# One more couple of up-projection blocks shares its P2 product, operand sums are queued behind weight splits, and the last norm's sums are gathered one product before their matmul

## The chip, the cores and the metric

The kernel runs on one core of a Trainium2 chip. The metric is the time of one execution in device microseconds (us). Before the change the median of three runs is 917.64 us (916.22 to 918.17).

## What is computed

One layer of a decoder trunk over 1024 tokens of width 1024, in float32. A normalised input goes through a projection into a pooling mixer and a gated recurrence, an output projection follows, then a squared-ReLU MLP of width 4096, a gated embedding, and a last norm:

```python
h = h + jnp.concatenate([y_pool, y_lru], axis=-1) @ w_out[l]
z = rms_norm(h, norm_mlp_g[l])
h = h + jnp.square(jax.nn.relu(z @ w_up[l])) @ w_down[l]
z = rms_norm(h, norm_ple_g[l])
gate = jax.nn.sigmoid(z @ w_ple_gate[l] + b_ple_gate[l])
h = h + gate * (p[l] @ w_ple_proj[l])
return rms_norm(h, norm_final_g)
```

The change lies in `z @ w_up` (the up-projection) and in the norm ahead of `w_ple_gate`.

## The kernel before

**Precision.** Each float32 operand is split into a rounded upper part (ScalarE, ACT in the profile, line L189) and a lower part, the remainder (VectorE, DVE, line L190). A product is three matmuls per block: upper by upper, upper by lower, lower by upper. A matmul that reads a lower part waits for its L190.

**The up-projection** is done in 16 blocks m = 0 to 15 of 256 output columns. Each block is a 2 by 2 block product by a seven-product scheme (Strassen's with Winograd's sums): P1 to P7, each 12 matmuls of 512 columns on 4 blocks of 128. P1 and P2 use the operands `y_wide`, P3 uses `y`, P4 to P7 use `a`. Two products of neighbouring blocks can again be made together by the same scheme, with halves: seven small products of 6 matmuls of 256 columns each (`sub_product`, L1020), in place of two products of 12 matmuls of 512. In the code this is a couple: `DOUBLES` lists the first blocks of the couples that make P4 together (3, 5, ... 13), `LATERS` those that make P2 together (6, 8, 10, 12). The second block of a couple runs `up_double`, in which the small products are woven between the block's own; all other blocks run `up_pair` with whole products.

A couple needs sums of its token operands (`double_operand`, L983 and L986, on DVE) and their splits, made once for all couples: n = 3, 1, 2 and 4, for P4 out of `a` and for P2 out of `y_wide`. Number 4 overwrites a quarter of the operand itself, so no whole P2 (or P4) can run behind it until it is restored. It also needs sums of its weights: for P4 in `double_weight`, for P2 in `later_sums`, which is issued behind the split of P6 of the couple's first block.

**What sets the order.** Python issues instructions with priorities, and a scheduler lays down one fixed order for each engine before the run. `issue_after(x)` keeps what is issued under it behind the instruction x in that order; `lowest[0]` is the newest lower split. Each engine then works through its own queue in order. The weights of a product live in four tiles (two tags of two buffers), so a weight can be split only when the product four weights before it has been made.

**The end of the kernel** (n = 0 to 7 in the loop over output blocks, first half of the tokens): each n is a projection of 6 matmuls and a gate of 24. The norm of the second half is made on the way. `Norm.add` squares and adds the 8 blocks, `Norm.gather` transposes and reduces them on DVE and splits the small result (L506, L507, L508, L509), one matmul by a block matrix spreads the sums (L519, written to `n2b_ps`), and `Norm.rstd` takes them on. Weights of the gate for blocks 4 to 7 are loaded into `wg_raw` and split on the same engines, into `a`.

Of the kernel before, what the change touches and what calls it, by code (L numbers as in the profile page):

```python
# [49 lines left out]
NPAIR = DFF // P // 2  # L50
# [14 lines left out]
def block_kernel(  # L65
# [48 lines left out]
    R = fixed("rstd", F32)  # L114
    start = pool.tile([P, 6 * S + NVEC + NT * S + 64], F32, name="t_h")
    t_all = start[:, : 6 * S].rearrange("p (i s) -> p i s", i=6)
    T = [t_all[:, i] for i in range(6)]
# [18 lines left out]
    def bank(name):  # L136
        return pd.tile([P, HALF], F32, tag="pd", name=name)
# [46 lines left out]
    lowest, upper = [], []  # L184
# [80 lines left out]
    FIRST_UP = "P6", "P7", "P4", "P5", "P1", "P2", "P3"  # L265
    UP = [(0, kind) for kind in FIRST_UP]
    DOUBLES = range(3, NPAIR - 1, 2)
    LATERS = range(6, NPAIR - 2, 2)

    def doubled(m):  # L270
        return "P4" if m - 1 in DOUBLES else "P2" if m - 1 in LATERS else None
# [4 lines left out]
    for m in range(1, NPAIR - 1):  # L276
        if doubled(m):
            n = second_alone(m)
# [678 lines left out]
    def copy(to, ps, fn=AF.Copy):  # L957
        nc.scalar.activation(by(to, ps), got(ps), fn)
# [30 lines left out]
    def double_operand(k, n):  # L989

        b11, b12, b21, b22 = ([f32(x) for x in quadrant(k, i, j)] for i in range(2) for j in range(2))
        to = apart(E[1][:, SECOND] if k == "P4" else H[6][:, FIRST])
        if n == 3:
            total(to, ((1, b12[0]), (-1, b22[0]), (1, b12[1]), (-1, b22[1])))
            split(to, *extra_parts(k, 0))
        elif n == 1:
            total(to, ((1, b11[0]), (-1, b12[0]), (1, b11[1]), (-1, b12[1])))
            split(to, *extra_parts(k, 1))
        elif n == 2:
            total(to, ((1, to), (1, b22[0]), (1, b22[1])))  # L1000
            split(to, *extra_parts(k, 2))
        else:
            total(to, ((-1, to), (1, b21[0]), (1, b21[1])))
            split(to, *quadrant(k, 0, 1))
# [86 lines left out]
    def up_fourth(m):  # L1091
# [4 lines left out]
        finish_up(m, cc)  # L1096
        leave_up()

    def up_double(m, k):

        before, own = (up_sums(x)[3 if k == "P4" else 1] for x in (m - 1, m))
# [21 lines left out]
        nc.scalar.activation(by(own[:, right], z[:, right]), got(z[:, right]), AF.Copy, scale=-1.0)  # L1123
        up_product(m, "P6", b, more=True)
        copy(c12, b)
        x = bank(f"ps_x_u{m}")[:, left]
        sub_product(k, x, w54[1], 4)
        copy(own[:, left], x)
# [32 lines left out]
    def up_pair(m):  # L1161
        if doubled(m):
            return up_double(m, doubled(m))
        cc, c11, c12, c21, c22 = up_sums(m)
        a, d = up_open(m)
        b = chains[m]
        leave_up()
        if m > DOUBLES[0]:
            pass
        elif m > 1:  # L1170
            up_fourth(m - 1)
        else:
            norm.rstd(R, [x for hs in HALVES for x in norm.sums(hs)], square=True)
            leave("hl")
            extra["P4"].extend(space("x", 2, F32R))
        up_product(m, "P6", b, more=True)
        copy(c12, b)
        if m > DOUBLES[0]:
            finish_up(m - 1, up_sums(m - 1)[0])
        up_product(m, "P2", a, more=True)  # L1180
        copy(c11, a, AF.Relu)
        for k, ns in (("P4", ((), (3,), (1, 2), (4,))), ("P2", ((), (), (), (3,), (), (1, 2, 4)))):
            for n in ns[m] if m < len(ns) else ():
                double_operand(k, n)
        up_product(m, "P3", d, more=True)
        take(c12, d, c12)
        if m == 1:
            finish_up(0, up_sums(0)[0])
            leave_up()
        up_product(m, "P7", b, more=True)  # L1190
        take(c22, b, c22)
        if m in DOUBLES:
            copy(c21, chains.pop(m))
# [202 lines left out]
    norm2 = Norm("n2", T[0], T[1:2])  # L1396
# [224 lines left out]
    for g, hs in enumerate(GROUPS):  # L1621
# [3 lines left out]
        for n, o in enumerate(ORDER[g]):  # L1625
# [21 lines left out]
            if g == 0 and n > 0:  # L1647
                for o in range(NT) if n == 1 else ():
                    norm2.add(H[o], SECOND)
                if n == 3:  # L1650
                    norm2.rstd(R, norm2.sums(SECOND, T[2][:, SECOND]))
                for o in LATER[n - 1]:
                    ple_in_normed(o, SECOND)
            if g == 1:
# [143 lines left out]
```

## Time and profile before

| what | value |
|---|---|
| median of 3 runs | 917.64 us (916.22 to 918.17) |
| the profiled execution, its own time | 918.25 us |
| its span, first to last instruction | 916.4 us |
| mean granted TensorE clock | 0.997 |
| busy: TensorE (PE) | 906.0 us, 99% |
| busy: VectorE (DVE) | 737.0 us, 80% |
| busy: ScalarE (ACT) | 514.2 us, 56% |
| stage of the up-projection, from the PE's rows | 224.97 to about 511 us |

A row of a timeline gives the start, the length, the engine, the line, the operation, what is written and read, the shape, how many instructions the row merges, and in brackets how long the engine sat idle before it and what ended that. Matmuls overlap, so the price of one is the distance from start to start, not its length. PEld is the weight load of the PE, which goes ahead of its matmul.

### The profile page before, as it was taken

Reading aid. Unit: us, or ns where it says so; the run is one execution under the profiler, and the core shown is the slowest. Engines: PE = TensorE matmul, PEld = TensorE weight load, DVE = VectorE, ACT = ScalarE, POOL = GpSimd, SP = SyncE. Lnnn points to the kernel's source line nnn. Section 1 sums busy time; section 2 is a strip of 40 time slices with the busy share of each in tenths; the row PEclk is TensorE's granted clock in tenths of the full one; section 3 lists DMA queues with packets and bytes.
Section 4 is the critical chain, followed back from the end, with each engine's and each line's share of the span. In section 5 each row is a group of like instructions: output and inputs, shape, how many; then the busy total and the mean of one; then the engine's idle time right before and its main releaser. Section 6 shows DMA issues by size and latency. Waiting matters only on the chain.

```text
span 916.4 us, 11820 instructions
## 1 busy us (share of the span) xinstructions
PE 906.0 (99%) x4401; PEld 794.0 (87%) x4401; DVE 737.0 (80%) x1004; ACT 514.2 (56%) x683; POOL 51.9 (6%) x76
## 2 busy tenths in 40 slices
PE   9999999999999999999999999999999999998996
PEld 7888888888888989999998888888888888887886
DVE  7999974668998667887887877799777589898876
ACT  6569892447565656666767554564343346475323
POOL 4400001000000000000000000000001001100001
PEclk9999999999999999999999999999999999999999
DMA  8210145435478667778685988366535355331353
GB/s 274 101 47 28 63 150 151 150 92 174 112 188 254 173 204 195 204 233 203 190 242 180 359 312 293 116 218 197 201 97 136 129 167 119 70 100 62 93 173 135
DMA packets 60328, 150.88 MB, mean 165 GB/s; under 512 B 5360, under 2 KB 10352, under 8 KB 60272
## 3 DMA queue, kind: packets, MB, share of 16 engines
q1 hardware_dynamic: 54288, 136.77, 45.3%
q0 software_dynamic: 4752, 12.59, 8.3%
q10 hardware_dynamic: 1232, 0.79, 0.4%
q8 instruction: 34, 0.56, 0.2%
q14 instruction: 22, 0.18, 0.1%
HBM read 110.27 MB, written 39.85 MB: 164 GB/s over the span
## 4 chain that ended last, share of the span: by engine, by line
PE 93%; DVE 4%; issue 1%; DMA 1%; ACT 0%; POOLq 0%; POOL 0%; ACTq 0%; DVEq 0%
PE ps_P_d L447 31%; PE ps_i L447 9%; PE ps_o L447 9%; PE ps_b_u L447 8%; PE ps_d_u L447 8%; PE ps_a_u L447 6%; PE ps_e L447 5%; PE ps_l L447 3%; PE ps_z_u L1020 3%; PE ps_e L1533 2%; PE ps_P_u L447 2%; PE ps_v_u L1020 1%; PE ps_l L644 1%; PE ps_x_u L1020 1%; PE ps_g L713 1%
## 5 line engine op out<-in xcount | busy, mean ns | idle before, releaser
L447 PE MATMUL ps_P_d<-a,wd_P_hi 128*128 128x512 f32 x880 | 261.7, 379 | 0.0
L447 PEld LDWEIGHTS ps_P_d<-a,wd_P_hi 128*128 128x128 f32 x880 | 166.3, 189 | 23.6
L447 PE MATMUL ps_P_d<-a,wd_P_lo 128*128 128x512 f32 x440 | 166.8, 379 | 0.0
L447 PEld LDWEIGHTS ps_P_d<-a,wd_P_lo 128*128 128x128 f32 x440 | 83.2, 189 | 11.8
L222 DVE TENSOR_TENSOR t_h<-t_h 128x512 f32<-128x512 f32 (+2 forms) x104 | 72.6, 708 | 14.1 <-ACT t_h L925 13.0
L190 DVE TENSOR_TENSOR wu_P<-t_h,wu_P 128x512 fp32r<-128x512 f32 x86 | 58.7, 686 | 30.8 <-ACT wu_P L189 30.7
L447 PE MATMUL ps_b_u<-a,wu_P 128*128 128x512 f32 x360 | 82.4, 379 | 0.0
L447 PEld LDWEIGHTS ps_b_u<-a,wu_P 128*128 128x128 f32 x360 | 66.6, 189 | 8.6
L190 DVE TENSOR_TENSOR a<-wd,a 128x1024 fp32r<-128x1024 f32 x56 | 67.3, 1220 | 2.3 <-ACT a L189 2.0
L189 ACT ACTIVATE wu_P<-t_h 128x512 fp32r<-128x512 f32 x86 | 53.3, 624 | 24.0 <-DVE t_h L222 10.6
L447 PE MATMUL ps_i<-a,wi_hi 128*128 128x512 f32 x256 | 66.1, 381 | 0.0
L189 ACT ACTIVATE a<-wd 128x1024 fp32r<-128x1024 f32 x56 | 58.3, 1051 | 9.3 <-PE ps_P_d L447 6.5
L899 DVE TENSOR_TENSOR t_h<-t_h,ps_P_d 128x512 f32<-128x512 f32 (+1 forms) x48 | 37.1, 772 | 30.5 <-PE ps_P_d L447 30.5
L447 PE MATMUL ps_a_u<-y_wide,wu_P 128*128 128x512 f32 x264 | 60.6, 379 | 0.0
L447 PEld LDWEIGHTS ps_a_u<-y_wide,wu_P 128*128 128x128 f32 x264 | 49.7, 189 | 7.0
L447 PEld LDWEIGHTS ps_i<-a,wi_hi 128*128 128x128 f32 x256 | 48.1, 189 | 8.0 <-PE ps_g L713 0.3
L189 ACT ACTIVATE wd_P_hi<-wd 128x1024 fp32r<-128x1024 f32 x24 | 25.3, 1054 | 50.0 <-PE ps_P_d L447 47.9
L447 PE MATMUL ps_d_u<-a,wu_P 128*128 128x512 f32 x180 | 41.3, 379 | 0.0
L447 PE MATMUL ps_d_u<-y,wu_P 128*128 128x512 f32 x180 | 41.3, 379 | 0.0
L447 PE MATMUL ps_i<-a,wi_lo 128*128 128x512 f32 x128 | 38.1, 379 | 0.0
L190 DVE TENSOR_TENSOR wd_P_lo<-wd,wd_P_hi 128x1024 fp32r<-128x1024 f32 x24 | 29.3, 1221 | 10.1 <-ACT wd_P_hi L189 10.1
L447 PEld LDWEIGHTS ps_d_u<-a,wu_P 128*128 128x128 f32 x180 | 33.3, 189 | 4.3
(307 smaller groups left out, 1731.8 us busy)
## 6 DMA issues: line engine op xcount, KB each, us to landing
wd<-act SPq DMA_DIRECT2D x56, 512.0 KB, 5.7
act<-t_h SPq DMA_DIRECT2D x48, 512.0 KB, 4.9
t_h<-in_w_up SPq DMA_DIRECT2D x30, 512.0 KB, 5.2
wd<-in_w_down SPq DMA_DIRECT2D x16, 512.0 KB, 6.7
t_h<-in_w_up POOLq DMA_DIRECT2D x15, 512.0 KB, 7.1
t_h<-in_xT SPq DMA_DIRECT2D x14, 512.0 KB, 4.6
wg_raw<-in_w_gate SPq DMA_DIRECT2D x10, 512.0 KB, 3.2
wi_raw<-in_w_in SPq DMA_DIRECT2D x9, 512.0 KB, 3.2
```

Of the source, the lines that this page charges most:

```text
L189: first = pin(nc.scalar.activation(hi, src, AF.Copy))
L190: lowest[:] = [pin((eng or nc.vector).tensor_tensor(lo, src, f32(hi), ALU.subtract)).ins]
L222: return nc.vector.tensor_tensor(to, x, y, op).ins
L447: ins = nc.tensor.matmul(ps, w, turns(z[:, hs]), start=first and z is zhi and w is whi, stop=last and w is wlo, skip_group_check=more,)
L644: nc.tensor.matmul(ps, kblk(w, o), turns(z[:, hs]), start=k == n == 0, stop=False)
L713: nc.tensor.matmul(x, w[r, o * P : (o + 1) * P], turns(z[r, at : at + HALF]), start=n == 0, stop=n == 2)
L899: (eng or nc.vector).tensor_tensor(to, to if y is None else y, x, ALU.add)
L1020: nc.tensor.matmul(ps, kblk(w, t), turns(z[:, t]), start=t == x == 0 and not more, stop=t == 1 and x == 2, skip_group_check=more,)
L1533: nc.tensor.matmul(pg, z, turns(quad[x == 1][:, k]), start=n == 0, stop=n == 3 * NT - 1, skip_group_check=True)
```

## The change

`LATERS` begins at 4 instead of 6, so that blocks 4 and 5 make P2 together as well: block 5 goes through `up_double` instead of `up_pair`, and blocks 4 and 5 have no whole P2 of their own. The operand sums for P2 have to be there two blocks earlier: n = 3 and 1 are made in block 3, n = 2 and 4 in block 4 (before: 3 in block 3, the rest in block 5). All operand sums, those of P4 too, are now issued behind the newest lower split. In the end stage the gather of the second norm's sums is issued at n = 2, its matmul stays at n = 3.

```diff
-    LATERS = range(6, NPAIR - 2, 2)
+    LATERS = range(4, NPAIR - 2, 2)
...
+    MADE = {"P4": {1: (3,), 2: (1, 2), 3: (4,)}, "P2": {3: (3, 1), 4: (2, 4)}}
+
+    def double_operands(m):
+
+        for k, ns in MADE.items():
+            for n in ns.get(m, ()):
+                with tc.issue_after(lowest[0]):
+                    double_operand(k, n)
+
     def up_double(m, k):
...
         up_product(m, "P6", b, more=True)
         copy(c12, b)
+        double_operands(m)
         x = bank(f"ps_x_u{m}")[:, left]
...
         up_product(m, "P2", a, more=True)
         copy(c11, a, AF.Relu)
-        for k, ns in (("P4", ((), (3,), (1, 2), (4,))), ("P2", ((), (), (), (3,), (), (1, 2, 4)))):
-            for n in ns[m] if m < len(ns) else ():
-                double_operand(k, n)
+        double_operands(m)
         up_product(m, "P3", d, more=True)
...
+                if n == 2:
+                    norm2.gather(SECOND, T[2][:, SECOND])
                 if n == 3:
-                    norm2.rstd(R, norm2.sums(SECOND, T[2][:, SECOND]))
+                    norm2.rstd(R, norm2.sums(SECOND))
```

How this moves instructions shows at three places.

**DVE, as block 0 of the up-projection begins.** The rows named wu_P are the lower splits of P1 (1869), P2 (1872) and P3 (1875) of block 0, y_124 is a token operand, and L986 is an operand sum.

```order
 L193 SCALAR_TENSOR_TENSOR y_124<-t_h,y_123 128x512
 L190 TENSOR_TENSOR a<-t_h,a 128x1024 x2
-L986 TENSOR_TENSOR t_h<-y_wide 128x512
-L986 TENSOR_TENSOR t_h<-t_h,y_wide 128x512 x2
 L190 TENSOR_TENSOR wu_P_1869<-wu_0_raw,wu_P_1869 128x512
+L193 SCALAR_TENSOR_TENSOR y_124<-t_h,y_123 128x512
 L190 TENSOR_TENSOR wu_P_1872<-wu_0_raw,wu_P_1872 128x512
-L193 SCALAR_TENSOR_TENSOR y_124<-t_h,y_123 128x512
 L190 TENSOR_TENSOR wu_P_1875<-rstd,wu_P_1875 128x512
```

Three operand sums of P2 (n = 3) stood ahead of the split of P1; they are gone from here, and one operand split moves between P1 and P2.

**DVE, at the change from block 3 to block 4.** Here wu4_P1, wu4_P5 and wu4_P6 are lower weight splits of block 4, wu3_d0 and wu3_d1 the first two of the P4 couple of blocks 3 and 4; L222 x2 forms parts of block 2's result. Before, from there to the split of d1:

```order
L222 TENSOR_TENSOR t_h_70<-t_h_70 128x512 x2
L190 TENSOR_TENSOR wu4_P1_2333<-t_h_70,wu4_P1_2333 128x512
L222 TENSOR_TENSOR t_h_70<-t_h_70 128x1024
L190 TENSOR_TENSOR wu3_d0_2349<-t_h_70,wu3_d0_2349 128x512
L222 TENSOR_TENSOR t_h_70<-t_h_70 128x256
L1045 TENSOR_TENSOR t_h_70<-ps_d_u3_2227,t_h_70 128x512
L190 TENSOR_TENSOR wu4_P5_2368<-t_h_70,wu4_P5_2368 128x512
L222 TENSOR_TENSOR t_h_70<-t_h_70 128x256
L222 TENSOR_TENSOR t_h_70<-t_h_70 128x512
L222 TENSOR_TENSOR t_h_70<-t_h_70 128x256
L1045 TENSOR_TENSOR t_h_70<-ps_b_u3_2244,t_h_70 128x512
L190 TENSOR_TENSOR wu3_d1_2386<-t_h_70,wu3_d1_2386 128x512
```

Now the same stretch has 22 instructions instead of 13. Its first half, up to the split x30 of the operand sum n = 3:

```order
L222 TENSOR_TENSOR t_h_70<-t_h_70 128x512 x2
L190 TENSOR_TENSOR a_68<-t_h_70,a_68 128x2x256
L222 TENSOR_TENSOR t_h_70<-t_h_70 128x1024
L986 TENSOR_TENSOR t_h_70<-y_wide_120 128x512
L190 TENSOR_TENSOR wu4_P1_2338<-t_h_70,wu4_P1_2338 128x512
L986 TENSOR_TENSOR t_h_70<-t_h_70,y_wide_120 128x512
L1045 TENSOR_TENSOR t_h_70<-ps_d_u3_2227,t_h_70 128x512
L986 TENSOR_TENSOR t_h_70<-t_h_70,y_wide_120 128x512
L190 TENSOR_TENSOR wu3_d0_2354<-t_h_70,wu3_d0_2354 128x512
L222 TENSOR_TENSOR t_h_70<-t_h_70 128x256
L190 TENSOR_TENSOR x30_1775<-t_h_70,x30_1775 128x512
```

And its second half, up to the split of d1 (x31 is the split of n = 1):

```order
L1045 TENSOR_TENSOR t_h_70<-ps_b_u3_2244,t_h_70 128x512
L986 TENSOR_TENSOR t_h_70<-y_wide_120 128x512
L190 TENSOR_TENSOR wu4_P5_2373<-t_h_70,wu4_P5_2373 128x512
L986 TENSOR_TENSOR t_h_70<-t_h_70,y_wide_120 128x512
L222 TENSOR_TENSOR t_h_70<-t_h_70 128x512
L986 TENSOR_TENSOR t_h_70<-t_h_70,y_wide_120 128x512
L222 TENSOR_TENSOR t_h_70<-t_h_70 128x256
L190 TENSOR_TENSOR wu4_P6_2409<-t_h_70,wu4_P6_2409 128x512
L190 TENSOR_TENSOR x31_1776<-t_h_70,x31_1776 128x512
L190 TENSOR_TENSOR wu3_d1_2392<-t_h_70,wu3_d1_2392 128x512
```

Ten instructions of 512 columns have come ahead of d1's split: six sums, three operand splits (a, x30, x31) and the split of P6; one L222 of 256 columns has gone behind it.

**DVE and PE at the last norm.** On DVE, sums is the small split result of the gather, a<-wg_6_raw the lower split of the gate's weights for block 6, and L1447 (now L1455) takes a gate's product.

```order
-L508 CAST sums_6190<-edge 128x16
-L1452 TENSOR_TENSOR t_h<-t_h 128x512
+L1459 TENSOR_TENSOR t_h<-t_h,ps_j_2_6610 128x512
+L508 CAST sums_6229<-edge 128x16
+L1460 TENSOR_TENSOR t_h<-t_h 128x512
+L509 TENSOR_TENSOR sums_6229<-edge,sums_6229 128x16
 L190 TENSOR_TENSOR a<-wg_6_raw,a 128x8x128
 L492 TENSOR_TENSOR t_h<-t_h 128x512
-L1447 TENSOR_TENSOR t_h<-ps_e_3_6618,rstd 128x512
-L509 TENSOR_TENSOR sums_6190<-edge,sums_6190 128x16
-L528 COPY edge<-n2b_ps_6669 128x16
```

L509, on which the matmul waits, stood behind the weight split, L492 and L1447; now it stands ahead of all three. On PE, before:

```order
L447 MATMUL ps_e_5_6730<-proj_6438,proj_6443 128x512
L447 MATMUL ps_e_5_6730<-ple_6194,a 128x512
L447 MATMUL ps_e_5_6730<-ple_6195,a 128x512
L447 MATMUL ps_e_5_6730<-ple_6194,a 128x512
L519 MATMUL n2b_ps_6669<-sums_6190,same 128x32
L447 MATMUL ps_j_4_6683<-proj_6436,proj_6440 128x512
```

And now:

```order
L447 MATMUL ps_e_3_6661<-ple_6239,wg_3_hi 128x512
L447 MATMUL ps_e_3_6661<-ple_6240,wg_3_hi 128x512
L447 MATMUL ps_e_3_6661<-ple_6239,wg_3_lo 128x512
L519 MATMUL n2b_ps_6708<-sums_6229,same 128x32
L447 MATMUL ps_j_4_6722<-proj_6475,proj_6479 128x512
L447 MATMUL ps_j_4_6722<-proj_6476,proj_6479 128x512
```

The nine matmuls of block 5 that went ahead of the sums' matmul now come behind it, after block 4's.

## The prediction

> **What bounds the kernel now.** I read the busy times first, then the waits of the PE, then the places of these waits.
>
> ```profile
> span 916.4 us, 11820 instructions
> PE 906.0 (99%) x4401; PEld 794.0 (87%) x4401; DVE 737.0 (80%) x1004; ACT 514.2 (56%) x683; POOL 51.9 (6%) x76
> PE n2b_ps L519 <- DVE sums L509: 2.5, 1, 2.5
> ```
>
> The PE is the bound: 906.0 of 916.4 us, and the last row, from the table of the PE's waits, is its only wait for data over 1 us: the matmul of the last norm's sums, once, 2.5 us. So this change can gain in three ways only: fewer matmul columns, a wait less, or a faster clock. I went to the wait in the PE's timeline.
>
> ```profile
> 826.86 1.46 PE L447 MATMUL ps_e<-proj,proj 128*128 128x512 f32 x6
> 828.16 0.81 PE L447 MATMUL ps_e<-ple,a 128*128 128x512 f32 x3
> 831.47 0.28 PE L519 MATMUL n2b_ps<-sums,same 128*128 128x32 f32 x1 [2.50 <-DVE sums L509]
> 831.60 1.99 PE L447 MATMUL ps_j<-proj,proj 128*128 128x512 f32 x6
> 833.38 11.16 PE L447 MATMUL ps_e<-ple,a 128*128 128x512 f32 x45
> 844.38 1.46 PE L447 MATMUL ps_j<-proj,proj 128*128 128x512 f32 x6
> ```
>
> The six matmuls ahead of the wait take 1.30 us from start to start (828.16 - 826.86), the six behind it 1.78. The windows of that second show why (columns: window, PE busy and its matmuls, granted clock, DMA share, GB/s):
>
> ```profile
> 832.00:833.00 1.00, 1.00 (x6) 0.78 0.80 324
> 833.00:834.00 1.00, 1.00 (x4) 0.50 0.00 0
> ...
> 835.00:836.00 1.00, 1.00 (x4) 0.51 0.00 0
> 836.00:837.00 1.00, 1.00 (x6) 1.00 0.00 0
> ```
>
> The clock drops to half about 1.1 us behind the wait and stays there for some 3.4 us. So the wait costs more than its row says. Why it lasts, DVE's timeline and one row of ACT tell:
>
> ```profile
> 826.58 0.17 DVE L508 CAST sums<-edge 128x16 fp32r<-128x16 f32 x1
> 826.70 0.69 DVE L1452 TENSOR_TENSOR t_h<-t_h 128x512 f32<-128x512 f32 x1
> 828.91 1.22 DVE L190 TENSOR_TENSOR a<-wg_raw,a 128x1024 fp32r<-128x1024 f32 x1 [1.51 <-ACT a L189]
> 830.65 0.68 DVE L1447 TENSOR_TENSOR t_h<-ps_e,rstd 128x512 f32<-128x512 f32 x1
> 831.25 0.17 DVE L509 TENSOR_TENSOR sums<-edge,sums 128x16 fp32r<-128x16 f32 x1
> 827.82 1.06 ACT L189 ACTIVATE a<-wg_raw 128x1024 fp32r<-128x1024 f32 x1 [2.27 <-DMA wg_raw<-in_w_gate]
> ```
>
> L508 is done at 826.75, but L509 stands behind a weight split whose data a DMA brings at 827.8. The second place is the start of the up-projection:
>
> ```profile
> 224.97 10.52 PE L447 MATMUL ps_P_u<-a,wu_P 128*128 128x512 f32 x48
> 235.33 5.74 PE L447 MATMUL ps_P_u<-y_wide,wu_P 128*128 128x512 f32 x24
> 240.91 2.75 PE L447 MATMUL ps_P_u<-y,wu_P 128*128 128x512 f32 x12
> 236.05 0.94 PEld L447 LDWEIGHTS ps_P_u<-y_wide,wu_P 128*128 128x128 f32 x5 [0.53 <-DVE wu_P L190]
> 235.33:240.91 5.58, 5.45 (x26) 1.00 0.46 87
> 233.26 0.69 DVE L986 TENSOR_TENSOR t_h<-y_wide 128x512 f32<-128x512 f32 x1
> 235.32 1.28 DVE L190 TENSOR_TENSOR wu_P<-wu_raw,wu_P 128x512 fp32r<-128x512 f32 x2
> 233.59 1.28 ACT L189 ACTIVATE wu_P<-wu_raw 128x512 fp32r<-128x512 f32 x2 [2.00 <-PE ps_P_u L447]
> ```
>
> 48 matmuls take 10.36 us, 0.2158 each, which is my price of a 512-column matmul. The next 24 should take 5.18 and take 5.58: the PE waits for the lower split of P1, and this short wait leaves the clock at 1.00 (fifth row).
>
> **The change, part by part.**
>
> *The last norm, -3.78.* From 826.86 to 844.38 are 17.52 us for 60 matmuls (6 + 3 + 6 + 45: 12.95) and n2b (831.60 - 831.47 = 0.13), 13.08 in all. So 4.44 us are lost: 2.66 standing (from 828.16 + 3 x 0.2158 = 828.81 to 831.47) and 1.78 at half clock. Now L509 comes straight behind L1452. That starts at 826.70, the next DVE instruction follows 0.60 later (830.65 to 831.25), so L509 ends at about 827.47 and n2b can start 0.05 later, as it does now. The PE, however, arrives earlier, since nine matmuls have gone behind n2b: at 826.86. It still waits 0.66 us. That is near the 0.40 to 0.53 at 235 which left the clock alone, far below 2.66, so I take no half clock: 4.44 - 0.66 = 3.78. Bounds: 4.44, if DVE moves forward more than the PE; 2.00 (2.66 - 0.66), if the slow clock comes all the same.
>
> [...]
>
> Is the gain kept to the end? Behind n2b the PE needs things that DVE may not have earlier:
>
> ```profile
> 853.93 0.69 DVE L190 TENSOR_TENSOR a<-t_h,a 128x512 fp32r<-128x512 f32 x1
> 864.22 0.17 DVE L509 TENSOR_TENSOR sums<-edge,sums 128x16 fp32r<-128x16 f32 x1
> 870.28 0.18 PE L519 MATMUL n_ps<-sums,same 128*128 128x32 f32 x1
> 858.63 0.59 PE L447 MATMUL ps_e<-a,wg_hi 128*128 128x512 f32 x2
> ```
>
> The last split of the second half's operand ends at 854.62; the PE would want the first of the eight at 858.63 - 3.78 = 854.85. The next norm's sums end at 864.39 and would be wanted at 866.5. Both hold even if DVE gains nothing, so the gain is kept.
>
> *The start of the up-projection, -0.40.* Without the three L986 (233.26 to 235.32) the split of P1 follows its upper part, which ACT has at 234.2, and ends near 234.9, before the PE's third matmul at 235.76. The next, P2's, gets an operand split ahead of it and ends near 236.2; the PE wants it 2.59 us behind 235.33, so nothing new is late. Bounds 0 and 0.40.
>
> *The couple, -0.50 of matmuls.*
>
> ```profile
> 307.31 2.76 PE L447 MATMUL ps_a_u<-y_wide,wu_P 128*128 128x512 f32 x12
> 323.52 2.75 PE L447 MATMUL ps_a_u<-y_wide,wu_P 128*128 128x512 f32 x12
> 351.52 0.83 PE L1020 MATMUL ps_z_u<-y_wide,wu_l 128*128 128x256 f32 x6
> 352.19 2.76 PE L447 MATMUL ps_d_u<-a,wu_P 128*128 128x512 f32 x12
> ```
>
> The first two rows are the products that go: 24 x 0.2158 = 5.18. Six small matmuls cost 0.67 (352.19 - 351.52), seven such groups 4.68. That a matmul of half the columns costs a little more than half is in it already.
>
> *The wait that it makes, +0.95.* The couple's sums are not free for DVE at the change from block 3 to 4. Rows of before:
>
> ```profile
> 289.92 1.42 DVE L222 TENSOR_TENSOR t_h<-t_h 128x512 f32<-128x512 f32 x2 [2.72 <-ACT t_h L925]
> 294.53 0.68 DVE L190 TENSOR_TENSOR wu_P<-t_h,wu_P 128x512 fp32r<-128x512 f32 x1
> 297.01 0.68 DVE L190 TENSOR_TENSOR wu_d<-t_h,wu_d 128x512 fp32r<-128x512 f32 x1
> 302.04 0.83 PE L1020 MATMUL ps_z_u<-x,wu_d 128*128 128x256 f32 x6
> 298.78 2.76 PE L447 MATMUL ps_d_u<-a,wu_P 128*128 128x512 f32 x12
> ```
>
> DVE cannot start earlier than 289.92, where it waits for ACT's squares. From there to the split of d1 (297.01) it goes on without a pause. Ten instructions of 0.60 come in and one of 256 columns (0.33) goes, so d1's lower part starts at 302.7 and ends at 303.4. The PE wants it after two small matmuls at 302.26, and one of P6, which the new order puts between, makes it 302.48: 0.9 late, with the 0.05 of the signal 0.95. P5's split (294.53) gets seven ahead of it, ends at 299.4 and is wanted at 299.21: 0.25 late, and lies inside the 0.95, since what the PE loses there it does not wait again. Behind d1 the same reckoning gives d2, d3 and the splits of block 5 0.1 to 3 us to spare, least for P5 of block 5. Bounds: 0, which is what every couple of before shows (PE idle 0.0 through all of them), and 2.0, if P5 of both blocks and d1 are late in full. I take the reckoned value, because both ends of it are rows of the same stretch. The added work of the couple on DVE (four sums of weights, smaller splits, additions, some 4 us over two blocks) is hidden by matmuls, as in the four couples of before; without that cover the delay is what the upper bound holds. On SP and POOL no transfer is added: the load of block 6's first weights goes behind a split of block 5's small products, as it does for the later couples.
>
> The sum: -3.78 - 0.40 - 0.50 + 0.95 = -3.73. The profiled execution took 918.25 us (1.85 more than its span) and would take 914.5. It lies 0.6 above the median of the runs, 917.64; from that I get **913.9 us**.
>
> **The rivals.**
>
> *No wait at d1, or none left at n2b.* For: no couple of before makes the PE wait. Against: DVE is busy without a pause from 289.9 on. Time: 917.64 - 4.68 = 912.9, and 912.3 with both.
>
> [...]
>
> *The gain is taken back behind n2b.* The PE runs 3.78 us ahead of a DVE that gains nothing, and waits at the second half's operand, 0.23 us from the edge, or at the next norm, 2.1 us from it. If DVE comes later than before by 2 us, both waits end late and some 2 us go: 916 to 917.
>
> *Slower: DVE falls behind for two blocks.* The wait at d1 grows until it is as long as the one at n2b and brings the half clock too, and P5 of block 5 follows it. Each then costs 4.44: -4.68 + 8.88 = +4.2, 921.8 us. It decides from where DVE is 1.7 us later than I reckon (2.66 - 0.95). For: no slack from 289.9 to about 317. Against: the splits of block 5 follow waits for the PE itself, so a delay gives DVE room.
>
> **How the numbers follow.** My forecast 0.60 (its own range 912.9 to 915.2), no new wait 0.14, half clock stays 0.12, taken back 0.08, slower 0.06. The low end, 912.2, is all bounds in favour and a little noise; the high end, 916.7, is the half clock with d1 at its upper bound (915.7 + 1.05). What is left out is most of the last two cases. A measurement of this kernel can tell about 0.2%, 1.84 us, from no change, so faster means below 915.8: the first two cases and two thirds of the third, 0.82. Same 0.12, slower 0.06.
>
> **What would show it.** In the profile after: the PE's wait at n2b 0.4 to 0.9 us instead of 2.5, and the clock at 1.00 from 826 to 840; no PEld wait for wu_P behind block 0's P4 to P7, and P1 and P2 there in 5.18 us; in blocks 4 and 5 small products from `y_wide`; between P5 and P6 of block 4 about 1 us in which the PE waits for a split of DVE's; the two blocks together about 0.45 us longer. A clock at half behind n2b, or a wait over 2 us in block 4, would make the prediction wrong.

## The result and the profile after

The kernel after takes 914.44 us (median of seven runs, 914.14 to 915.40), the kernel before 917.64 (seven runs, 915.98 to 919.98). The ratio is 0.9966, with a 95% interval of 0.9953 to 0.9979: faster, by 0.34% or 3.2 us in the medians, against 3.73 predicted (913.9). One run of a later kernel, the one with the moved fetch, took 1369.16 us at a granted clock of 0.655 and is left out of that kernel's numbers. The profiled execution went from 918.25 to 914.14 us, its span from 916.4 to 912.4.

First the head of the page of the kernel after.

```profile
span 912.4 us, 11874 instructions
PE 903.5 (99%) x4419; PEld 792.5 (87%) x4419; DVE 742.0 (81%) x1015; ACT 517.3 (57%) x688; POOL 51.8 (6%) x76
```

The PE is busy 2.5 us less, with 18 more matmuls (42 small for 24 whole). Its waits for data (engine, line, waited for: us, times, longest):

```profile
PE n2b_ps L519 <- DVE sums L509: 0.6, 1, 0.6
PE ps_z_u L1020 <- DVE wu_d L190: 0.2, 1, 0.2
```

The wait of 2.5 us at the last norm's sums is 0.6 now, and a small one at a split `wu_d` is new. The PE's timeline at the last norm, then two windows (columns: window, its length, busy us and count of PE, PEld, DVE, ACT and POOL, granted clock, DMA share, GB/s):

```profile
826.03 0.38 PE L447 MATMUL ps_e<-ple,wg_lo 128*128 128x512 f32 x1
826.99 0.28 PE L519 MATMUL n2b_ps<-sums,same 128*128 128x32 f32 x1 [0.58 <-DVE sums L509]
827.12 1.54 PE L447 MATMUL ps_j<-proj,proj 128*128 128x512 f32 x6
828.50 5.34 PE L447 MATMUL ps_e<-ple,a 128*128 128x512 f32 x24
833.68 1.46 PE L447 MATMUL ps_e<-proj,proj 128*128 128x512 f32 x6
834.97 5.34 PE L447 MATMUL ps_e<-ple,a 128*128 128x512 f32 x24
840.15 1.46 PE L447 MATMUL ps_j<-proj,proj 128*128 128x512 f32 x6
```

```profile
827.00:828.00 1.00, 1.00 (x5) 0.92 (x6) 1.00 (x2) 0.51 (x1) 0.00 (x0) 1.00 0.00 0
833.00:834.00 1.00, 1.00 (x6) 0.86 (x6) 1.00 (x3) 0.21 (x1) 0.00 (x0) 1.00 0.00 0
```

From the end of the gate ahead of it (826.03 + 0.2158 = 826.25) to 840.15 the same 60 matmuls take 13.90 us; in the kernel before they took 17.52. So 3.62 go. The PE stands 0.74 (826.25 to 826.99), and the clock stays at 1.00.

At the start of the up-projection, in the PE's timeline, P1 and P2 of block 0 take 5.18 us (239.73 - 234.55), as 24 matmuls should; before it was 5.58.

```profile
224.19 10.52 PE L447 MATMUL ps_P_u<-a,wu_P 128*128 128x512 f32 x48
234.55 5.34 PE L447 MATMUL ps_P_u<-y_wide,wu_P 128*128 128x512 f32 x24
239.73 2.75 PE L447 MATMUL ps_P_u<-y,wu_P 128*128 128x512 f32 x12
```

Blocks 4 and 5 in the PE's timeline; block 6 begins with the last row:

```profile
294.34 2.75 PE L447 MATMUL ps_a_u<-y_wide,wu_P 128*128 128x512 f32 x12
296.93 0.83 PE L1020 MATMUL ps_z_u<-a,wu_d 128*128 128x256 f32 x6
297.60 3.13 PE L447 MATMUL ps_d_u<-a,wu_P 128*128 128x512 f32 x12
300.56 0.83 PE L1020 MATMUL ps_z_u<-a,wu_d 128*128 128x256 f32 x6
301.29 0.49 PE L1020 MATMUL ps_z_u<-x,wu_d 128*128 128x256 f32 x2
301.62 0.38 PE L447 MATMUL ps_b_u<-a,wu_P 128*128 128x512 f32 x1
302.25 0.71 PE L1020 MATMUL ps_z_u<-x,wu_d 128*128 128x256 f32 x4 [0.25 <-DVE wu_d L190]
...
330.67 2.75 PE L447 MATMUL ps_a_u<-y_wide,wu_P 128*128 128x512 f32 x12
```

The same two starts in the kernel before:

```profile
295.52 2.75 PE L447 MATMUL ps_a_u<-y_wide,wu_P 128*128 128x512 f32 x12
...
331.29 2.75 PE L447 MATMUL ps_a_u<-y_wide,wu_P 128*128 128x512 f32 x12
```

They take 36.33 us, before 35.77. So the couple costs 0.56. The new waits are two: P5 takes 2.96 (300.56 - 297.60) where 12 matmuls take 2.59, 0.37 lost at its lower split; and from 300.56 to 302.25 stand the first eight small matmuls and one of P6 (8 x 0.1113 + 0.2158 = 1.11) and 0.58 more, at the split of d1. With 0.11 in small pieces that is 1.06 us of waits against 0.50 saved.

The profiled executions differ by 0.78 already at 224 us, ahead of everything that the change touches. Thirteen profiles of this study in which nothing ahead of it differs start the up-projection between 223.98 and 225.04 us, so this is no effect of the change.

### The profile page after: what moved, and what is told of

Same layout as the page of the kernel before. It is cut to its first block, busy times and chain, and to the rows that moved or that the text cites. A ratio compares the mean times of both kernels' runs of the same rounds, so it can differ in the third digit from the quotient of the medians.

```text
span 912.4 us, 11874 instructions
## 1 busy us (share of the span) xinstructions
PE 903.5 (99%) x4419; PEld 792.5 (87%) x4419; DVE 742.0 (81%) x1015; ACT 517.3 (57%) x688; POOL 51.8 (6%) x76
## 4 chain that ended last, share of the span: by engine, by line
PE 92%; DVE 4%; issue 2%; DMA 1%; ACT 0%; POOLq 0%; POOL 0%; ACTq 0%; DVEq 0%
PE ps_P_d L447 31%; PE ps_i L447 9%; PE ps_o L447 9%; PE ps_d_u L447 8%; PE ps_b_u L447 8%; PE ps_a_u L447 5%; PE ps_e L447 5%; PE ps_z_u L1020 3%; PE ps_l L447 3%; PE ps_P_u L447 3%; PE ps_e L1541 2%; PE ps_v_u L1020 2%; PE ps_l L644 1%; PE ps_x_u L1020 1%; PE ps_g L713 1%
## 5 line engine op out<-in xcount | busy, mean ns | idle before, releaser
L222 DVE TENSOR_TENSOR t_h<-t_h 128x512 f32<-128x512 f32 (+2 forms) x104 | 72.6, 708 | 11.6 <-ACT t_h L925 10.4
L190 DVE TENSOR_TENSOR wu_P<-t_h,wu_P 128x512 fp32r<-128x512 f32 x84 | 57.4, 686 | 27.8 <-ACT wu_P L189 27.6
L190 DVE TENSOR_TENSOR a<-wd,a 128x1024 fp32r<-128x1024 f32 x56 | 67.3, 1220 | 2.6 <-ACT a L189 2.3
L447 PE MATMUL ps_a_u<-y_wide,wu_P 128*128 128x512 f32 x240 | 55.1, 379 | 0.0
L447 PEld LDWEIGHTS ps_a_u<-y_wide,wu_P 128*128 128x128 f32 x240 | 45.3, 189 | 6.4
L190 DVE TENSOR_TENSOR wd_P_lo<-wd,wd_P_hi 128x1024 fp32r<-128x1024 f32 x24 | 29.3, 1221 | 10.1 <-ACT wd_P_hi L189 10.1
```

The source lines that it names most:

```text
L190: lowest[:] = [pin((eng or nc.vector).tensor_tensor(lo, src, f32(hi), ALU.subtract)).ins]
L222: return nc.vector.tensor_tensor(to, x, y, op).ins
L447: ins = nc.tensor.matmul(ps, w, turns(z[:, hs]), start=first and z is zhi and w is whi, stop=last and w is wlo, skip_group_check=more,)
```

## The experiments

### The last norm alone

Theory: standing time and half clock are one loss and both go. Rival: the half clock is not the wait's doing.

```diff
 (kernel before)
+                if n == 2:
+                    norm2.gather(SECOND, T[2][:, SECOND])
                 if n == 3:
-                    norm2.rstd(R, norm2.sums(SECOND, T[2][:, SECOND]))
+                    norm2.rstd(R, norm2.sums(SECOND))
```

> The kernel before, with the last norm's sums gathered one product ahead of their matmul and nothing else changed. Theory (the lost 4.44 us are one thing: standing time and the half clock that it brings): the time falls by 3.6 to 3.8 us, from 917.6 to about 913.9 (ratio 0.9959), the PE waits 0.6 us at the matmul of the sums and the granted clock is 1.00 behind it. Rival (the half clock has another cause and stays): the time falls by about 2.0, to 915.6, and some 3 us behind the matmul stand at half clock. Rival (the gain is taken back further on): 916 or more, with a wait of over 1 us at the second half's products or at the last norm but one.

Measured: 913.74 us (913.38 to 914.47, 12 runs) against 917.21 (34 runs); ratio 0.9973 (0.9961 to 0.9984). Its PE timeline at the last norm:

```profile
826.56 0.28 PE L519 MATMUL n2b_ps<-sums,same 128*128 128x32 f32 x1 [0.51 <-DVE sums L509]
826.70 1.54 PE L447 MATMUL ps_j<-proj,proj 128*128 128x512 f32 x6
```

As the theory has it: a wait of 0.5, a clock of 1.00 behind it, 3.5 us less in the median. The two rivals fall. But this kernel is 0.7 faster than the whole change, and its runs lie within 1.1 us of each other, while the 34 runs of the kernel before beside it reach from 913.93 to 918.66.

### The up-projection alone

```diff
 (kernel after)
-                if n == 2:
-                    norm2.gather(SECOND, T[2][:, SECOND])
                 if n == 3:
-                    norm2.rstd(R, norm2.sums(SECOND))
+                    norm2.rstd(R, norm2.sums(SECOND, T[2][:, SECOND]))
```

> The kernel after, with the last norm's sums and their matmul together again, as in the kernel before; the couple and the queued sums stay. Theory: -0.40 at the start of the up-projection and +0.45 to +0.56 in blocks 4 and 5 cancel, so 917.6 to 917.9 (ratio 1.0000 to 1.0003), and the wait of 2.5 us and the half clock behind it are there again. Rival (the couple is worth its 0.50 and the waits in block 4 cost nothing at the end): 916.7 (0.9990). Rival (the couple costs more than the profile shows, which would explain a median gain of 3.2 beside 4.0 in the profiled execution): 918.4 (1.0009).

Measured: 915.05 us (914.39 to 916.10, 12 runs) against 917.21; ratio 0.9986 (0.9976 to 0.9996). None of the three expectations. The last norm has the same order on DVE and PE as in the kernel before, and yet:

```profile
829.30 0.28 PE L519 MATMUL n2b_ps<-sums,same 128*128 128x32 f32 x1 [0.77 <-DVE sums L509]
```

A wait of 0.77 in the place of 2.50, and no half clock. Something made the wait of the kernel before long which this kernel, unchanged there, doesn't meet. The 34 runs of the kernel before say that it doesn't always meet it either: 11 lie between 913.9 and 915.3, four between 915.7 and 916.7, 19 between 917.0 and 918.7. Their mean granted clocks part them too: 0.998 or 0.999 in all fifteen runs of the first two groups, 0.996 or 0.997 in all nineteen of the third, so by them only the third has the half clock. The profile from which I predicted was one of the third group.

### What makes the wait long: a fetch of the PE's program in the load's tail

L509 stands behind a weight split (L190), which needs the load of `wg_raw`. In the kernel before that load was issued at 822.95 and ACT could start on it at 827.82, 4.87 later; in the kernel after it takes 3.35. Its row in the chain that ended last, then the DMA view of the kernel before, 825 to 828 us (GB/s in 40 slices of 0.075 us; then a queue's packets, MB and share of 16 engines' time):

```profile
822.95 4.84 DMA wg_raw<-in_w_gate
...
GB/s 218 328 328 437 382 328 546 219 437 55 0 0 0 0 0 0 0 0 0 0 0 55 0 0 0 0 0 55 0 0 0 0 0 0 0 0 0 0 0 0
...
q8 instruction: 1, 0.02, 2.0%
```

The load is over by 825.9 but for two packets at 826.6 and 827.0. Among them lies one packet of the queue `instruction`, 16 KB, which holds one of the 16 DMA engines for 0.96 us (2.0% of 16 x 3 us). Two late packets, about as late as this fetch is long: I take it that it stood in their way. (By the trace's packet records the fetch lasts from 825.66 to 826.62 and the first late packet starts at 826.61. That they share one engine is inferred; no record names it.) The same shows on the load ahead of this one. In five profiles a fetch falls in its time, and it takes 4.5 us (the kernel after, with the fetch at 818.6), 5.0 (the up-projection alone) and, in three kernels told below, 4.4 (the sums spread otherwise), 4.2 (the matmul of the sums moved) and 4.0 (the fetch moved); in the kernel before and with the norm's part alone, where none does, 3.2 and 3.3. Whose program it is I take from its step: the kernel before has 34 such fetches (17.6 to 30.6 us apart), and between one and the next lie 102 to 152 matmuls of the PE, 127 on average, with about as many weight loads, but 23 to 66 instructions of DVE and 16 to 41 of ACT. The one ahead of this lies 27.3 us and 127 matmuls earlier. So it should be the PE's (an inference; no record names the engine), and its place should move with the number of matmuls: the couple adds 18, and the fetch came 6 to 7 us earlier, at 818.6 to 819.3, ahead of the load. (18 matmuls are 3.9 us; the rest is another shift of about 3 us that the kernel with the norm's part alone shows without any more matmuls, its fetch at 822.1. What sets that shift is open.)

To test it, the kernel before with more matmuls at its very start:

```diff
 (kernel before)
-    for _ in range(WARM):
+    for _ in range(5):
         nc.tensor.matmul(ps_l[2][0][1][:, :HALF], warm, wide, start=True, stop=True)
+    for _ in range(24):
+        nc.tensor.matmul(ps_l[2][0][1][:, :16], warm, wide[:, :16], start=True, stop=True)
```

> The kernel before, with its eight warming matmuls at the very start (512 columns, on constants) replaced by five of them and 24 of 16 columns: 21 matmuls more, which shift every later 16 KB fetch of the PE's own program by some 42 instructions, 4.5 us, and change nothing else. Theory (the long wait at the last norm's sums comes from such a fetch, which in the profiled execution of the kernel before falls on 825 to 826 us and holds up the tail of the gate weights' load): the fetch now falls on 820 to 822, the load lands in about 3.3 us instead of 4.8, the wait is 0.8 to 1.0 us, no half clock follows, and all runs lie at 914 to 915.5 like the lower third of the runs of the kernel before; the start may cost up to 1 us. Rival (the two groups of times of the kernel before have another cause): runs on both sides of 916 as before, median 917.

Measured: 915.3 to 917.2 us in eleven runs, median 916.06; ratio 0.9995 (0.9983 to 1.0008). The fetch falls on 820.1, the load takes 3.2 us, and the wait is

```profile
830.90 0.28 PE L519 MATMUL n2b_ps<-sums,same 128*128 128x32 f32 x1 [0.93 <-DVE sums L509]
```

with the clock at 1.00 behind it. The profile is as the theory says. The times are not the 914 to 915.5 that were expected, since the altered start costs 1 to 2 us (the up-projection begins at 225.97), and they alone would not decide: their spread is 1.9 us, less than half of the 5.0 of the 18 runs of the kernel before beside them.

Then the kernel before itself, once more:

> The kernel before, unchanged, profiled once more. Its times so far lie in groups: near 914.4, near 916.3 and near 917.7. Theory: they differ in two things only, whether a fetch of the PE's own program falls on the tail of the gate weights' load (1.5 us more standing at the last norm's sums) and whether the standing time then fills enough of one of the clock's windows of 3.41 us (1.7 us more). So either the load lands in about 3.3 us with the fetch elsewhere, the wait is 0.8 to 1.0 and the time near 914.4; or the fetch falls on the last microsecond of the load, the load takes 4.6 to 5.0, the wait is 2.3 to 2.6, and the time is near 916 or 917.7 according to the clock. Rival: a long wait without the fetch in the load, or a short one with it.

Measured: 914.69 us, span 912.8. (The 3.41 us of its theory are the length of the half clock in the kernel before, 832.56 to 835.97 in the trace's records of the clock.) Its PE timeline, then ACT's start on the load, then the same DMA view as above:

```profile
827.75 0.81 PE L447 MATMUL ps_e<-ple,a 128*128 128x512 f32 x3
829.60 0.28 PE L519 MATMUL n2b_ps<-sums,same 128*128 128x32 f32 x1 [1.04 <-DVE sums L509]
```

```profile
825.94 1.06 ACT L189 ACTIVATE a<-wg_raw 128x1024 fp32r<-128x1024 f32 x1 [0.90 <-DMA wg_raw<-in_w_gate]
```

```profile
GB/s 164 55 55 55 0 0 218 0 0 0 0 0 0 0 0 0 0 0 0 0 0 0 0 0 0 0 0 0 0 0 0 0 0 0 0 0 0 0 0 0
...
q8 instruction: 1, 0.02, 2.0%
```

The same program, 3.6 us faster than its profiled execution of before. Neither of the two ways that I had written down is quite it: the fetch is at 825.45 here too (the 218 in the seventh slice), but the load was issued 0.5 earlier (822.45) and had just ended. So it is a race of the load's last packets with the fetch, which in these two profiles the 0.5 us of the issue decided. Lost, the wait is 2.50 and the PE stands 2.66; won, it is 1.04 and the PE stands 1.20 (828.40 to 829.60). 914.4 + 1.46 = 915.9 and + 1.78 of half clock = 917.7 lie in the second and the third group. (No run of the second group was profiled: that it is the long wait without the half clock rests on this sum and on the granted clocks of its runs.)

### When the half clock comes

Standing times of 0.74 to 1.20 left the clock alone, 2.66 did not. Two kernels were to find the edge. The first, with two unused additions on DVE between the halves of the sums:

```diff
 (kernel after, Norm.gather of the last norm)
             keep(nc.vector.tensor_copy(hi, few))
+            for _ in range(2):
+                nc.vector.tensor_tensor(t, self.acc[:, hs], self.acc[:, hs], ALU.add)
             ins = nc.vector.tensor_tensor(lo, few, f32(hi), ALU.subtract)
```

> The kernel after, with two additions of 512 columns each (their result is not used) put on DVE between the upper and the lower half of the last norm's sums, 0.6 us each. So the PE stands about 0.75 + 1.20 = 1.95 us at the matmul of the sums. Question: which standing time brings the half clock; 0.93 does not (the kernel after with its last norm as before), 2.66 does (the kernel before). Theory A (half clock from about 2 us on): clock 0.50 for some 3 us behind the matmul and 917.4. [...]

Measured: 914.42 us. It missed its aim: the scheduler put three matmuls of a later product ahead of the sums, and the PE stood 1.23 us. Clock 1.00. The second makes the PE stand near the end, where its order is fixed:

```diff
 (kernel after, gate_opened)
         gate_products(i, pg, range(1))
+        for _ in range(10 if i == 1 else 0):
+            pin(nc.vector.tensor_tensor(T[4][:, SECOND], b_row, b_row, ALU.add))
```

> The kernel after, with ten additions of 512 columns (their result is not used) put on DVE ahead of the second token slice's bias addition, near the end, where the PE's order is fixed: the PE has nothing else to do and stands still for about 2.0 us near 887 us, once. Question: which standing time brings the half clock, between 1.2 us (which left it at 1.00) and 2.66 (which brought 3.4 us of 0.50). Theory A (about 2 us are enough): a stretch of some 3.4 us at 0.50 begins about 1 us behind the end of the stall, and the kernel is 3.7 us slower than the kernel after, 918. Theory B (it takes more): clock 1.00 throughout, 2.0 us slower, 916.4.

Measured: 920.5 us. The additions took 0.72 each in a row, so the PE stood 3.8 us and not the 2.0 aimed at, from 886.2 to 890.05 (its timeline, then three windows):

```profile
890.05 2.93 PE L1567 MATMUL ps_e<-proj,proj 128*128 128x512 f32 x6 [3.66 <-DVE ps_e L1552]
```

```profile
889.00:890.00 1.00, 0.00 (x0) 0.00 (x0) 1.00 (x3) 0.00 (x0) 0.00 (x0) 1.00 0.63 116
890.00:891.00 1.00, 0.95 (x2) 0.84 (x3) 0.96 (x2) 0.00 (x0) 0.00 (x0) 0.51 0.56 92
893.00:894.00 1.00, 1.00 (x5) 0.83 (x5) 0.00 (x0) 0.67 (x2) 0.00 (x0) 0.78 0.57 213
```

The half clock lasts from 890.0 to 893.4, 3.4 us again, but it begins with the end of the standing time, not 1.1 us later. What may tell the cases apart is a grid. By the trace's records of the clock it stays at half for 3.413 us in the kernel before, and the next change comes 78.51 us later, 23 times 3.413. The stretch of full clock that begins at 6.54 us there lasts 826.03 us, the one that begins at 4.95 in the kernel after 904.53: 242 and 265 times, to within 0.1 us. A kernel made for another question (POOL, below) stood twice, and only the second time brought the half clock. Its PE timeline, and its windows:

```profile
235.97 2.64 PE L447 MATMUL ps_P_u<-a,wu_P 128*128 128x512 f32 x11 [2.78 <-DVE a L190]
...
308.16 1.65 PE L1021 MATMUL ps_z_u<-a,wu_d 128*128 128x256 f32 x6 [3.89 <-ACT ps_v_u L1125]
```

```profile
233.00:234.00 1.00, 0.19 (x1) 0.00 (x0) 1.00 (x2) 0.00 (x0) 1.00 (x2) 1.00 1.06 248
234.00:235.00 1.00, 0.00 (x0) 0.00 (x0) 1.00 (x1) 0.15 (x1) 0.82 (x1) 1.00 1.06 244
235.00:236.00 1.00, 0.03 (x1) 0.03 (x1) 1.00 (x2) 0.48 (x1) 0.00 (x0) 1.00 1.14 223
...
304.00:305.00 1.00, 0.27 (x2) 0.00 (x0) 1.00 (x2) 0.00 (x0) 0.94 (x1) 1.00 0.00 0
...
306.00:307.00 1.00, 0.00 (x0) 0.00 (x0) 1.00 (x3) 1.00 (x3) 0.00 (x0) 0.85 0.00 0
307.00:308.00 1.00, 0.00 (x0) 0.00 (x0) 1.00 (x3) 1.00 (x3) 0.00 (x0) 0.50 0.00 0
```

It stood 2.78 us, 233.19 to 235.97, at full clock throughout; and 3.89 us from 304.27, with half clock from 306.70 on (0.85 in the window means 0.30 us at half), while it was still standing. It lasts to about 313.5, twice 3.413: the windows from 307 to 313 show 0.50, and the twelve matmuls from 310.88 to 314.78 take 3.90 us in place of 2.59 (the end is an estimate from them). Count lengths of 3.413 us back from 306.70: one runs from 303.29 to 306.70 and has the PE idle for 2.43 us; 21 of them earlier a line falls on 235.02, if the grid holds, and parts the first standing time into 1.83 and 0.95. In the kernel before the half clock begins at 832.56 (0.78 in its window), so the length ahead of it runs from 829.15, with the PE idle to 831.47: 2.32 us. So, as far as one case of each kind shows: behind a length of 3.41 us with 2.3 idle us in it, or 2.4, the next was at half clock, behind one with 1.8 (by the grid) it was not, and a standing time of 2.8 that lay across a line cost nothing more than itself. In the POOL kernel the PE stood for 1.46 us, at half clock, of the length that begins at 306.70, and the next was at half too. That the clock goes by such a grid is an inference from these records. The edge between 1.8 and 2.3 stays open.

### The couple: its waits

First, the sums of the couple's four operands spread otherwise, with the one whose product comes last made last:

```diff
 (kernel after)
-    MADE = {..., "P2": {3: (3, 1), 4: (2, 4)}}
+    MADE = {..., "P2": {3: (1,), 4: (2, 4), 5: (3,)}}
```

> The kernel after, with the couple's operand sums spread otherwise: the second in block 3, the third and the fourth in block 4, the first (its product comes last) in block 5, instead of two in block 3 and two in block 4. Theory (the two waits in block 4, 0.4 at P5 and 0.5 at the second small product, are there only because DVE has the sums of two operands ahead of these weight splits): both waits go, blocks 4 and 5 together take 0.9 to 1.0 us less, 913.5 (ratio to the kernel before 0.9955). Rival (the work is only moved, and block 5's splits are late instead): a wait of 0.5 us or more in block 5 and 914.2 to 914.6 (0.9964). Rival (the wait comes from ACT or from a DMA, not from DVE's queue): the waits stay as they are.

(In this kernel the sums number 3 read a quarter that number 4 has overwritten, so the last small product multiplies another operand; instructions and sizes are the same.) Measured: 914.51 us (913.92 to 915.40, 12 runs), ratio 0.9976 (0.9964 to 0.9987). The waits at P5 and d1 are gone, and blocks 4 and 5 take 35.96 (295.01 to 330.97) in place of 36.33, but the PE now waits at the couple's last small product, 309.90, for DVE's L1045 on the bank that it goes on adding to (0.35 listed, 0.72 at the weight loads). The rival in its time, but not in its place: the lateness moved on within block 4 and not into block 5, which begins at 313.24.

Next, with three of the four in block 4 (and the matmul of the sums moved, which the section after this one tells):

```diff
-    MADE = {..., "P2": {3: (3, 1), 4: (2, 4)}}
+    MADE = {..., "P2": {3: (3,), 4: (1, 2, 4)}}
```

> The kernel after (five couples) with the matmul of the sums later and the couple's operands made otherwise: the sums of one operand in block 3 and of three in block 4, instead of two and two. Theory (the two waits in block 4, 0.4 and 0.5 to 0.6, come from the second operand's sums in DVE's queue there): they go, blocks 4 and 5 take 36.33 - 1.0 = 35.3 us instead of 35.77 without the couple, and the time is 913.77 - 1.0 = 912.8. Rival (the work moves the lateness into block 5): a wait of 0.3 us or more there and 913.4 or more.

Measured: 913.49 us (913.27 to 913.79, 7 runs), ratio 0.9965 (0.9951 to 0.9980). Blocks 4 and 5 take 36.38 (294.30 to 330.68), no gain, and the wait is in block 5, at its P5:

```profile
316.62 2.43 PE L447 MATMUL ps_d_u<-a,wu_P 128*128 128x512 f32 x10 [0.74 <-DVE wu_P L190]
```

Then a block earlier instead:

```diff
-    MADE = {..., "P2": {3: (3, 1), 4: (2, 4)}}
+    MADE = {..., "P2": {2: (3,), 3: (1,), 4: (2, 4)}}
```

> The same with all additions on DVE, but the sums of one of the two operands moved from block 3 to block 2 (2, 3, then two in block 4). DVE stands idle for 1.6 + 1.9 + 1.4 us in block 3 in the kernel after. Theory (there is room a block earlier): 2.4 us of DVE's work leave the front of block 4, no wait is left there nor in block 5, blocks 4 and 5 in 35.3 us, 912.8. Rival (the splits of block 3 become late instead, or block 5's do): blocks 3 to 5 together gain less than 0.5, 913.3 or more.

Measured: 913.32 us (913.00 to 914.01, 8 runs), ratio 0.9957 (0.9943 to 0.9972). Block 3 doesn't suffer (18.13 us, as in the kernel after), blocks 4 and 5 take 35.87, and one wait is left, in block 4 at the same small product as in the first spread; block 5 begins with the third row:

```profile
294.62 2.75 PE L447 MATMUL ps_a_u<-y_wide,wu_P 128*128 128x512 f32 x12
...
309.52 0.91 PE L1020 MATMUL ps_v_u<-x,wu_d 128*128 128x256 f32 x6 [0.35 <-DVE t_h L1045]
312.85 2.75 PE L447 MATMUL ps_a_u<-y_wide,wu_P 128*128 128x512 f32 x12
...
330.49 2.75 PE L447 MATMUL ps_a_u<-y_wide,wu_P 128*128 128x512 f32 x12
```

The best of the three spreads makes the couple cost 0.10 in place of 0.56 (35.77 without it). In the kernel after DVE goes on without a pause from 288.7 to 323.7, through all of block 4 and into block 5, so a sum that no longer stands ahead of one instruction the PE waits for stands ahead of another.

Last, the additions on POOL:

```diff
 (kernel after, the matmul of the sums moved; double_operand)
+        eng = nc.gpsimd if k == "P2" and n in (1, 2, 3, 4) else nc.vector
 ...
-            total(to, ((1, b12[0]), (-1, b22[0]), (1, b12[1]), (-1, b22[1])))
+            total(to, ((1, b12[0]), (-1, b22[0]), (1, b12[1]), (-1, b22[1])), eng)
```

> The kernel after with the matmul of the last norm's sums later (as tried before: 913.77, blocks 4 and 5 in 36.32 us), and the ten additions for the couple's four operands on POOL, which is busy 6% of the span, instead of DVE. Theory (the couple loses more than it saves only because its ten additions, 0.6 us each, stand in DVE's queue between blocks 3 and 5): the waits at P5 and at the second small product go, blocks 4 and 5 take 35.3 us, and the time is 912.8. Rival (POOL is too slow for it, or its additions hold up the loads of the up weights that POOL issues, or DVE is slowed beside it): a wait of 0.5 us or more in blocks 3 to 5, 913.5 or more.

Measured: 922.16 us (920.96 to 923.71, 6 runs), ratio 1.0054 (1.0033 to 1.0075): slower, by the rival. POOL's rows grouped (busy, mean ns), and a row of DVE and one of ACT beside them:

```profile
L986 POOL TENSOR_TENSOR t_h<-t_h,y_wide 128x512 f32<-128x512 f32 x7 | 10.3, 1468 | 1.9 <-DVE x L190 1.5
...
233.12 3.93 DVE L190 TENSOR_TENSOR a<-t_h,a 128x1024 fp32r<-128x1024 f32 x2
...
305.69 0.63 ACT L189 ACTIVATE x<-t_h 128x512 fp32r<-128x512 f32 x1 [1.83 <-POOL t_h L986]
```

An addition takes 1.47 us there (0.60 on DVE), and beside POOL's additions some of DVE's own instructions are longer: these two splits, which begin beside an addition that runs from 233.25 to 234.82, take 3.93 us, 2.36 in the kernel after. What slows them is not shown. The PE lost 2.8 and 3.9 us at the two places shown above: at the first behind DVE's longer splits, at the second behind ACT, whose queue had stood 1.83 us at a split until POOL had the sum for it.

### The wait that is left, and the couple left out

The matmul of the last norm's sums behind the next product's projections:

```diff
 (kernel after)
                 ple_proj(hs, o, pj)
+                if g == 0 and n == 4:
+                    norm2.rstd(R, norm2.sums(SECOND))
+                    for x in LATER[2]:
+                        ple_in_normed(x, SECOND)
                 ple_gate(g, hs, o, pg)
 ...
-                if n == 3:
-                    norm2.rstd(R, norm2.sums(SECOND))
-                for o in LATER[n - 1]:
+                for o in LATER[n - 1] if n != 3 else ():
```

> The kernel after, with the matmul of the last norm's sums put behind the next product's six short projections instead of ahead of them (1.29 us later on the PE). Theory: the remaining wait of 0.75 us from end to start goes in full, since the sums are ready 0.75 late; 913.7 (ratio to the kernel before 0.9957). The norm's result comes about 0.5 us later; the second half's last split, 3 us early in the kernel after, covers that. Rival (the later result makes the second half's products wait): 914.4 or more, with a wait at the first of them.

Measured: 913.77 us (913.28 to 914.55, 11 runs), ratio 0.9971 (0.9959 to 0.9982), 0.67 below the kernel after. No wait is left there. And the same without the couple, on the kernel before, with the gather and the queued sums:

```diff
 (kernel before, with the gather at n == 2 and the matmul as above)
             for n in ns[m] if m < len(ns) else ():
-                double_operand(k, n)
+                with tc.issue_after(lowest[0]):
+                    double_operand(k, n)
```

> The kernel before (four couples, not five) with the other two parts of the change and one more step: operand sums queued behind the weight splits, the last norm's sums gathered a product earlier, and their matmul behind the next product's short projections. Theory (the couple costs about 0.5 more than it saves, the queued sums save 0.40, the later matmul saves the remaining 0.5 us of wait): 913.74 - 0.40 - 0.51 = 912.8, below the kernel after by 1.6. Rival (the median gap of 0.7 between the kernel after and the norm's part alone is not the couple's): 913.4 or more. It differs from the norm's part alone by the queued sums and the later matmul.

Measured: 913.13 us (912.50 to 913.36, 6 runs), ratio 0.9958 (0.9943 to 0.9974). Its PE waits for no data at all over 0.2 us; blocks 4 and 5 take 35.77 (294.14 to 329.91), and block 0's P1 and P2 5.18. It lies 1.3 below the kernel after (914.44) and 0.64 below the same kernel with the couple (913.77; both from other sets of runs), which agrees with the 0.56 of the trace: the couple as it stands is a loss. (The intervals of the two ratios overlap, so it is the trace that says so.) This is the fastest version of the study, with the early spread of the couple's sums (913.32) next to it; the two cannot be told apart.

## Why the prediction was right, and where it was not

- **The last norm, -3.78.** In the profiled executions 3.62: the PE waits 0.74 where 0.66 was forecast, at full clock. That both parts of the loss come from the wait was right: behind waits of 0.51 us (the norm's part alone) and 0.58 (the kernel after) the clock is at 1.00. The 915.7 in the high end of the range takes off only 2.00 here (917.64 - 2.00 - 0.40 - 0.50 + 0.95), for a half clock that has another cause than the wait and stays; no run shows that. The reason given for no half clock, the length of the standing time, is only half of it: 0.74 us left the clock at 1.00, but so did 2.78 in the POOL kernel. What failed is a step that the text doesn't even state: that the 4.44 us are lost in every execution. The row of ACT's wait for the DMA (827.82) showed a load that took 4.87 us, and I took it as its duration. It had lost a race with a fetch of program code. In another profiled execution of the kernel before the PE stands 1.20 us without half clock, and the same edit would be worth about 0.46 there (1.20 - 0.74, an estimate). The median gain came out near the sum because more than half of the runs of the kernel before are of the long kind; the prediction didn't know of the groups, so that much of it was luck.
- **The start of the up-projection, -0.40.** Measured 0.40.
- **The couple, -0.50 and +0.95.** Together +0.56 in the trace, +0.45 forecast. The waits are where they were put, at P5 and d1 of block 4, but shared out 0.37 and 0.58 instead of 0.25 and 0.70, and 0.11 in small pieces comes on top.
- **The gain is kept behind n2b.** It is: the second half's last split ends at 851.47, and the PE wants the first at 854.40, 3 us later, since DVE moved forward too. That rival had no ground.
- **The slower rival** (DVE a further 1.7 us late in block 4) did not occur. The POOL kernel shows that a standing time of this kind brings the half clock here too (3.9 us, half clock from 306.70), but there the PE stood behind ACT and POOL; that DVE's queue alone would do it is not shown.
- **From the sum to the time.** The median is 0.5 above 913.9. The step that failed is the carrying over of 0.6 between profiled execution and median: after the change the profiled execution (914.14) lies 0.3 below the median. Profiled execution against profiled execution, 914.5 was forecast; 0.78 of the start came as a gift, 0.27 of norm and couple was missed, and somewhat over 0.1 was not located.
- **What made the gain.** Not the sum of the parts. The norm's part alone gives 3.5 us in the median; the up-projection's part, which costs about 0.2 by its own trace, alone gives 2.2, because its fetch comes at 819.3 and no longer in this load's tail; 18 more matmuls are 3.9 of the 6.3 us by which it moved.

## What to carry to other kernels

Before a long wait is priced, look at the spread of the runs: where the same program's times fall into groups (here near 914.4, 916.3 and 917.7), one profile shows one of them, and the transfer behind the wait may have been late by accident. An instruction that the bound engine waits for should not stand in a queue behind one that waits for a transfer; mending that made the time here both shorter (913.74 against 917.21 us) and steadier (1.1 us from the lowest run to the highest against 4.7). Work moved within a stretch in which its engine has no pause moved most or all of the wait with it; the most was gained by work moved to where the engine stood idle, here a block earlier (0.46 us in the two blocks, against 0.37 and none).

## What was not expected of the hardware

- A fetch of 16 KB of program, by its step the PE's, one of 34 in 916.4 us, held one DMA engine for 0.96 us, and a load of the gate's weights that met one took 4.0 to 5.0 us (six cases), not 3.2 or 3.3. Matmuls added ahead of it moved it: 21 at the start brought it from 825.7 to 820.1.
- The recorded changes of the granted clock in two profiles lie whole multiples of 3.413 us apart (1, 23, 242 and 265): 2.3 idle us within one such length brought 3.4 us at half clock, while a standing time of 2.8, parted by the grid, if it holds, into 1.8 and 1.0, brought none.
- POOL's additions of 512 columns took 1.47 us, and some of DVE's instructions beside them took longer: two splits 1.7 times as long (3.93 us against 2.36).
